# Zero rows of the latent heads' rope queries: eight ScalarE writes become eight GpSimd subtractions

## The chip, the cores and the metric

The kernel runs on one core of one Trainium2 chip. The metric is the time of one execution on the device, in microseconds (us). A core has five engines that run beside each other, each working through its own list in order: TensorE (PE, with PEld for its weight loads), VectorE (DVE), ScalarE (ACT), GpSimd (POOL) and SyncE (SP), which here issues the DMA transfers. An engine that waits for another engine's result holds up everything behind it on its own list.

## The reference

The program is a trunk of two layers over 256 latent and 256 context tokens of width 2048. The first layer joins neighbourhood attention (8 heads) with multi-head latent attention (8 heads); the second is a bidirectional gated DeltaNet. Only the latent heads matter here. With `cq` and `ckv` two normed projections of rank 512, each head computes

```
q  = rmsnorm(cq) @ w_qb          # per head: 128 columns qn, 64 columns qr
kv = rmsnorm(ckv) @ w_kvb        # per head: 128 columns kn, 128 columns v
s  = (qn . kn + rope_2d(qr) . kr) * scale      # kr: one 64-column key for all heads
o  = softmax(s) @ v
```

## The kernel before

Tokens lie along the free axis (512 columns: 256 latent, 256 context), features along the 128 partitions. Every product of fp32 data is made of three fp32r products: the operands are split into a high part (a cast on ACT, line 77 for weights) and a low part (a subtraction on DVE, line 78), and `dense` (lines 90 to 92) multiplies high by high, high by low and low by high. Weights come by DMA into four `raw` buffers.

The tile framework puts the instructions of each engine in an order of its own: it simulates the program with its own costs and lets each engine take what is ready. A change of one instruction can so move others that it has nothing to do with.

The place of the change is between the last neighbourhood head and the first latent head. In the order of the code:

- `na7 = na_head(7)` computes q, k and v of the last neighbourhood head from the layer's input `hx`. Its v product is the last reader of `hx`.
- `cx = parts_tile("cx")` takes over the buffer of `hx`. Its first half `ch` holds the high and low parts of the normed `cq` and `ckv`, eight pieces of 128x512: the high parts are cast on ACT (line 468), the low parts are subtracted on DVE (line 469). Its second half `qr` holds the rope queries of the eight heads.
- `cr.release()` gives back the buffer `craw` that lines 468 and 469 read. The pool `mr2` takes its place, and with it the three `mraw` buffers into which `adaln` loads the modulation weights of the second layer (`dn_wm`), in tiles of 512 KB. So the first of these loads waits for the last subtraction of line 469. Their products are `pmod` (line 141), two rows of TensorE's list for each tile, 16 for each of the chunks 2, 3 and 8; `macc` (line 147) and `pmt` (line 150) read a finished chunk out.
- `attend(*na7)` is the attention of head 7: scores `sp` (line 365), maximum `mx`, exponential `pr` (line 392), transposes `pt` (line 398), products `po`, in two passes (`s`).
- Then comes the loop over `j` in 0 to 3, in which the change lies. Each `j` computes the rope queries of two heads with 12 products, which read the first four pieces of `ch`, writes zeros, and calls `roped`, which scales (line 449), permutes on TensorE (`pp`, line 451), combines on DVE (lines 453 to 455) and writes the rows of each head (lines 357 and 358).

Two heads share the 128 partitions of a rope query tile. The key `kr` stands in both halves. So for each head one half of the rows of `qr` has to be zero, and line 481 writes these zeros: it reads `ones`, multiplies by 0 and writes 64 partitions x 1024 columns, twice for each `j`. The first reader of these rows is `sp<-kr,cx` of the first latent head.

Of the kernel before, what the change touches and what calls it, by code (L numbers as in the profile page):

```python
# [10 lines left out]
AF = mybir.ActivationFunctionType  # L11
ALU = mybir.AluOpType
# [6 lines left out]
T = 512  # L19
# [7 lines left out]
def trunk_kernel(ctx: ExitStack, tc: tile.TileContext, g):  # L27
    nc = tc.nc
    V, A, PE, P = nc.vector, nc.scalar, nc.tensor, nc.gpsimd
# [8 lines left out]
    def mm_tile():  # L38
        return mmp.tile([128, T], F32, name="mm", tag="mm")
# [4 lines left out]
    def cst(name, shape, src=None):  # L44
        t = const.tile(shape, F32, name=name, tag=name)
        if src is not None:
            nc.scalar.dma_start(t, src)
        return t
# [3 lines left out]
    ones = cst("ones", [128, 128])  # L52
# [32 lines left out]
    def dense(ps, w, off, kt, xh, xl, k0=0, sl=slice(0, T), first=True, last=True):  # L85
        for k in range(kt):
            c = off + k * 128
            wh, wl = w[c // 1024]
            c = slice(c % 1024, c % 1024 + 128)
            PE.matmul(ps, wh[:, c], xh[:, k0 + k, sl], start=first and k == 0, stop=False)  # L90
            PE.matmul(ps, wh[:, c], xl[:, k0 + k, sl], start=False, stop=False)  # L91
            end = PE.matmul(ps, wl[:, c], xh[:, k0 + k, sl], start=False, stop=last and k == kt - 1)  # L92
        return end.ins
# [225 lines left out]
    with tc.tile_pool(name="ab", bufs=2, reuse_waits="tile") as tp, \  # L319
# [124 lines left out]
        def roped(p, scale, parts_of):  # L444
            out = tp.tile([128, T], F32, name="rope", tag="rope", bufs=1)
            if scale == 1.0:
                A.copy(out, p)
            else:
                A.mul(out, p, scale)
            pp = ps.tile([128, S], F32, name="pp", tag="tr", bufs=TR)  # L450
            PE.matmul(pp, perm, out[:, :S], start=True, stop=True)
            t = tp.tile([128, S], F32, name="rtmp", tag="mtmp")
            V.tensor_tensor(t, pp, sinT, op=ALU.mult)
            V.tensor_tensor(out[:, :S], out[:, :S], cosT, op=ALU.mult)
            V.tensor_tensor(out[:, :S], out[:, :S], t, op=ALU.add)
            for r, hi, lo in parts_of:
                both(hi, lo, out[r])
# [5 lines left out]
        ch, qr = cx[:, 0], cx[:, 1]  # L463
        for i, gain in enumerate((q_gain, kv_gain)):
            for k in range(4):
                j = 4 * i + k
# [7 lines left out]
        rows = slice(0, 64), slice(64, 128)  # L474
        attend(*na7)
        w = load_split(g["ab_wqr"])
        for j in range(4):
            p = mm_tile()
            dense(p, w, j * 512, 4, ch, ch[:, 8:])
            for e in range(2):  # L480
                A.activation(qr[rows[1 - e], 4 * j + 2 * e:4 * j + 2 * e + 2],
                             ones[rows[1 - e], 0:1].unsqueeze(2).broadcast_to([64, 2, T]), AF.Copy, scale=0.0)
            roped(p, MLA_SCALE, [(rows[e], *[qr[rows[e], 4 * j + 2 * e + i] for i in range(2)]) for e in range(2)])
        for h in range(8):
            w = load_split(g["ab_wb"][h], 1536)
# [154 lines left out]
    with tc.tile_pool(name="dn", bufs=2, reuse_waits="tile") as tp, \  # L640
# [579 lines left out]
        for st in range(-2, 64 + LAG):  # L1220
            i, n = st // 4, st % 4
            j, m = (st - LAG) // 4, (st - LAG) % 4
# [196 lines left out]
def _program(arrays):  # L1419
    import concourse.bacc as _bacc  # L1420
    import concourse.tile as _tile

    nc = _bacc.Bacc("TRN2", target_bir_lowering=False, num_devices=1)
    g = {n: nc.dram_tensor(n, a.shape, F32, kind="ExternalInput").ap() for n, a in arrays.items()}
    g["out"] = nc.dram_tensor("out", (128, KT, S), F32, kind="ExternalOutput").ap()
    with _tile.TileContext(nc, schedule_with_timeline_sim=True) as tc:
        trunk_kernel(tc, g)
    return nc
# [11 lines left out]
```

## Time and profile before

| | us |
|---|---|
| median of 3 runs | 2490.44 (2487.42 to 2492.72) |
| the profiled execution | 2493.04 |
| its span on the core | 2491.2 |
| busy: PE / DVE / ACT / POOL | 2428.2 / 1762.8 / 1105.6 / 161.1 |

The profile is one execution. Its time is 1.8 us more than its span, and 2.6 us above the median of the runs. Times in the rows are counted from the start of the span. Busy times of PE overlap at their ends, since matmuls are pipelined.

### The profile page before, as it was taken

How to read it: one execution, taken by the hardware profiler on the slowest of the kernel's cores; microseconds unless marked ns; L12 is line 12 of the kernel's file. 1: busy time of each engine (PE TensorE's matmuls, PEld its weight loads, DVE VectorE, ACT ScalarE, POOL GpSimd, SP SyncE). 2: the span in 40 equal slices, each digit the busy share in tenths (PEclk: the TensorE clock that was granted, in tenths of full speed). 3: DMA queues.
4: the chain of work that ended last, by engine and by line, in shares of the span. 5: the costliest groups of instructions: out<-in, count | busy, mean ns of one | idle time of the engine just before them, and what ended most of it. 6: DMA issues, size and time to landing. Idle time of an engine off the chain costs nothing.

```text
span 2491.2 us, 42483 instructions
## 1 busy us (share of the span) xinstructions
PE 2428.2 (97%) x16110; PEld 1963.1 (79%) x16110; DVE 1762.8 (71%) x3538; ACT 1105.6 (44%) x2446; POOL 161.1 (6%) x165
## 2 busy tenths in 40 slices
PE   6999999999989999999999999999999999999998
PEld 4557888888858878858998989987777777777787
DVE  4654678883356687856998988885777777777765
ACT  4223332333254432257565655634444544445453
POOL 0000000000000000020011101000000000012000
PEclk9999999999999999999999999999999999999999
DMA  8872645542253366664665666774343333336454
GB/s 252 282 277 87 200 154 172 169 157 84 88 187 110 102 198 204 226 210 136 195 173 158 179 178 180 204 201 108 87 116 103 115 112 98 106 100 184 148 193 141
DMA packets 254940, 397.24 MB, mean 159 GB/s; under 512 B 122257, under 2 KB 163857, under 8 KB 254609
## 3 DMA queue, kind: packets, MB, share of 16 engines
q1 hardware_dynamic: 253584, 393.00, 52.0%
q8 instruction: 127, 2.08, 0.3%
q10 hardware_dynamic: 1152, 1.54, 0.2%
q14 instruction: 77, 0.62, 0.1%
HBM read 356.94 MB, written 35.39 MB: 157 GB/s over the span
## 4 chain that ended last, share of the span: by engine, by line
PE 88%; issue 5%; DMA 3%; DVE 2%; ACT 1%; SPq 0%; POOL 0%; DVEq 0%; POOLq 0%; ACTq 0%
PE mm L90 21%; PE mm L91 20%; PE mm L92 20%; PE pks L1033 3%; PE pmod L141 3%; PE ptr L1045 2%; PE sp L365 2%; PE mm L105 2%; PE po L365 1%; DMA mraw<-dn_wm 1%; PE ptr L1078 1%; PE psu L1064 1%; PE pks L1064 1%; PE pt L398 1%; PE mm L107 1%
## 5 line engine op out<-in xcount | busy, mean ns | idle before, releaser
L90 PE MATMUL mm<-hx,whi 128*128 128x512 f32 (+1 forms) x2304 | 843.7, 366 | 2.3 <-ACT t L664 2.2
L91 PE MATMUL mm<-hx,whi 128*128 128x512 f32 (+1 forms) x2304 | 820.6, 356 | 2.5 <-issue 2.5
L92 PE MATMUL mm<-hx,wlo 128*128 128x512 f32 (+1 forms) x2304 | 819.4, 356 | 0.6 <-DVE wlo L78 0.6
L77 ACT CAST whi<-raw 128x1024 fp32r<-128x1024 f32 (+2 forms) x346 | 338.6, 980 | 701.4 <-PE mm L91 502.3
L78 DVE TENSOR_TENSOR wlo<-raw,whi 128x1024 fp32r<-128x1024 f32 (+2 forms) x346 | 394.3, 1142 | 204.3 <-ACT whi L77 198.2
L90 PEld LDWEIGHTS mm<-hx,whi 128*128 128x128 f32 x2304 | 438.8, 190 | 106.3 <-issue 27.0
L92 PEld LDWEIGHTS mm<-hx,wlo 128*128 128x128 f32 x2304 | 438.6, 190 | 65.1 <-issue 4.2
L91 PEld LDWEIGHTS mm<-hx,whi 128*128 128x128 f32 x2304 | 438.8, 190 | 61.4 <-issue 9.2
L177 DVE SCALAR_TENSOR_TENSOR lacc<-mraw,cond,lacc 128x512 f32<-128x512 f32 x300 | 208.6, 746 | 0.7 <-DMA mraw<-dn_wm 0.7
L585 DVE SCALAR_TENSOR_TENSOR acc<-cin,taps,acc 128x508 f32<-128x508 f32 (+3 forms) x256 | 187.2, 731 | 20.3 <-ACT acc L576 17.2
L105 PE MATMUL mm<-hx,whi 128*128 128x512 f32 x480 | 173.1, 404 | 0.1
L1055 DVE SCALAR_TENSOR_TENSOR vl<-ptr,egm,vh 128x128 fp32r<-128x128 f32 x224 | 64.7, 346 | 95.1 <-ACT rf L1052 37.9
L107 PE MATMUL mm<-hx,wlo 128*128 128x256 f32 x457 | 128.4, 281 | 1.3 <-DVE wlo L1139 1.2
L141 PE MATMUL pmod<-mraw,cond 128*32 128x512 f32 (+2 forms) x640 | 98.4, 508 | 28.1 <-DMA mraw<-ab_wm 18.8
L1139 DVE TENSOR_TENSOR wlo<-raw,whi 128x1024 fp32r<-128x1024 f32 x84 | 102.5, 1221 | 13.5 <-ACT whi L1131 13.4
L105 PEld LDWEIGHTS mm<-hx,whi 128*128 128x128 f32 x480 | 88.9, 188 | 24.5 <-issue 5.0
L816 DVE SCALAR_TENSOR_TENSOR outer<-L,bv,X 128x31 f32<-128x31 f32 (+15 forms) x248 | 99.4, 401 | 6.4 <-POOL X L811 0.5
L90 PE MATMUL mm<-gx,whi 128*128 128x512 f32 x256 | 100.3, 394 | 3.4 <-DVE x1B L515 2.4
L599 ACT ACTIVATE ac<-acc 128x128 f32<-128x128 f32 x160 | 37.4, 300 | 144.2 <-DVE acc L585 144.1
L91 PE MATMUL mm<-gx,whi 128*128 128x512 f32 x256 | 100.4, 392 | 0.5 <-DVE gx L503 0.5
L92 PE MATMUL mm<-gx,wlo 128*128 128x512 f32 x256 | 99.8, 391 | 0.0
L1049 ACT ACTIVATE vh<-ptr,egm 128x128 fp32r<-128x128 f32 x224 | 71.3, 374 | 57.1 <-PE ptr L1045 55.2
(301 smaller groups left out, 3648.5 us busy)
## 6 DMA issues: line engine op xcount, KB each, us to landing
raw<-dn_w SPq DMA_DIRECT2D x194, 512.0 KB
mraw<-dn_wm SPq DMA_DIRECT2D x96, 512.0 KB
mraw<-ab_wm SPq DMA_DIRECT2D x88, 512.0 KB
raw<-ab_w SPq DMA_DIRECT2D x66, 512.0 KB
raw<-dn_wo SPq DMA_DIRECT2D x64, 512.0 KB
raw<-ab_wo SPq DMA_DIRECT2D x32, 512.0 KB
raw<-ab_w SPq DMA_DIRECT2D x32, 256.0 KB
spt<-sp SPq DMA_DIRECT2D x64, 128.0 KB
```

The source lines that it names most:

```text
L77: A.copy(hi[:, :m], raw[:, :m])
L78: V.tensor_tensor(lo[:, :m], raw[:, :m], hi[:, :m].bitcast(F32), op=ALU.subtract)
L90: PE.matmul(ps, wh[:, c], xh[:, k0 + k, sl], start=first and k == 0, stop=False)
L91: PE.matmul(ps, wh[:, c], xl[:, k0 + k, sl], start=False, stop=False)
L92: end = PE.matmul(ps, wl[:, c], xh[:, k0 + k, sl], start=False, stop=last and k == kt - 1)
L105: PE.matmul(p2, wh[:, c], x[:, :, k0 + k], start=start, stop=stop)
L107: PE.matmul(p2[:, 0], wl[:, c], x[:, 0, k0 + k], start=False, stop=False)
L141: PE.matmul(pmod[32 * q:32 * q + 32, :m], cond[:, 4 * kg + q, :], raw[c // 1024][:, half + c % 1024:half + c % 1024 + m], start=kg == 0, s ...
L177: V.scalar_tensor_tensor(acc[:, s], raw[:, q], cond[:, k, s:s + 1], acc[:, s], op0=ALU.mult, op1=ALU.add)
L585: V.scalar_tensor_tensor(o3[:, :, i0:i1], p3[:, :, i0 + d:i1 + d], taps[:, ch, t:t + 1], o3[:, :, i0:i1], op0=ALU.mult, op1=ALU.add)
L816: V.scalar_tensor_tensor(o, L[:, rows, k:k + 1].broadcast_to([128, n, m]), bv[:, k:k + 1], X[:, k:k + 1, cols].broadcast_to([128, n, m]), ...
L1139: V.tensor_tensor(w, raws[j], h.bitcast(F32), op=ALU.subtract)
```

## The change

The zeros are written by GpSimd: `ones - ones`, with the same rows and the same shape of 64x1024 (its line number is 482 in the changed kernel), instead of ACT's copy with scale 0.

```diff
             for e in range(2):
-                A.activation(qr[rows[1 - e], 4 * j + 2 * e:4 * j + 2 * e + 2],
-                             ones[rows[1 - e], 0:1].unsqueeze(2).broadcast_to([64, 2, T]), AF.Copy, scale=0.0)
+                one = ones[rows[1 - e], 0:1].unsqueeze(2).broadcast_to([64, 2, T])
+                P.tensor_tensor(qr[rows[1 - e], 4 * j + 2 * e:4 * j + 2 * e + 2], one, one, op=ALU.subtract)
```

On ACT's list, between the casts of `cx` and the scaling of the first rope query (`rope<-mm`), the rows read, with - for before and + for now:

```order
 L468 CAST cx<-craw 128x512 x8
-L481 ACTIVATE cx<-ones 64x1024 x6
 L357 CAST vt<-pv 128x512
-L481 ACTIVATE cx<-ones 64x1024
-L392 ACTIVATE pr,sm<-sp,mx 128x512
-L481 ACTIVATE cx<-ones 64x1024
-L392 ACTIVATE pr,sm<-sp,mx 128x512
+L392 ACTIVATE pr,sm<-sp,mx 128x512 x2
 L449 ACTIVATE rope<-mm 128x512
```

The eight zero writes are gone from between the casts and the two exponentials of head 7.

On GpSimd's list, between the modulation of the first layer and that of the second (`hx<-mh,hx`; `rs` belongs to a norm):

```order
 L208 TENSOR_TENSOR rs<-ms,half 128x4
 L243 TENSOR_TENSOR hx<-mh,hx 128x512 x11
-L208 TENSOR_TENSOR rs<-ms,half 128x4 x3
+L208 TENSOR_TENSOR rs<-ms,half 128x4 x2
+L482 TENSOR_TENSOR cx<-ones 64x1024 x8
+L208 TENSOR_TENSOR rs<-ms,half 128x4
 L243 TENSOR_TENSOR hx<-mh,hx 128x512 x11
```

The eight writes stand there in one piece; only the first has a wait, for TensorE.

On TensorE's list, what follows the products of `j` = 0 and 1 was before:

```order
L141 MATMUL pmod<-mraw,cond 32x512 x4
L365 MATMUL sp<-kT,qT 128x256 x3
L398 MATMUL pt<-ident,pr 128x128 x4
L141 MATMUL pmod<-mraw,cond 32x512 x2
L365 MATMUL sp<-kT,qT 128x256 x3
```

Now the second pass's scores and the twelve products of `j` = 2 stand there, and behind these:

```order
L398 MATMUL pt<-ident,pr 128x128 x8
L141 MATMUL pmod<-mraw,cond 32x512 x4
L365 MATMUL po<-PT,vt 128x256
L141 MATMUL pmod<-mraw,cond 32x512 x2
L398 MATMUL pt<-ident,pr 128x128 x2
L365 MATMUL po<-PT,vt 128x256 x11
```

So the first modulation products moved behind the scores, the products of `j` = 2 and eight transposes. Before the second `pp` (the permutation of `j` = 1) TensorE had ten tiles of `pmod` and now has eight; up to the first scores of the first latent head it had 16 and now has 15. DVE's list is unchanged from the splits of the weights through the eight subtractions of line 469. Farther on the lists differ again in small pieces, mostly at the start of the second layer, where ACT's list now holds two more loads of function tables.

## Rows read from the trace of the kernel before

**Rows 1.** The page, part 1: busy time, share of the span, instructions.

```profile
PE 2428.2 (97%) x16110; PEld 1963.1 (79%) x16110; DVE 1762.8 (71%) x3538; ACT 1105.6 (44%) x2446; POOL 161.1 (6%) x165
```

**Rows 2.** Busy time by stretch; last three columns: granted clock, DMA share, GB/s.

```profile
690.00:700.00 10.00, 5.74 (x24) 4.05 (x23) 6.41 (x12) 9.92 (x14) 0.00 (x0) 1.00 0.36 118
700.00:710.00 10.00, 9.40 (x36) 4.43 (x36) 4.28 (x11) 5.67 (x12) 0.00 (x0) 0.83 0.76 265
710.00:720.00 10.00, 9.42 (x51) 4.49 (x50) 4.27 (x11) 1.70 (x5) 0.00 (x0) 1.00 0.53 166
720.00:730.00 10.00, 8.10 (x38) 3.67 (x38) 5.63 (x11) 4.61 (x7) 0.00 (x0) 1.00 0.70 226
...
1140.00:1150.00 10.00, 8.67 (x90) 7.84 (x89) 6.30 (x10) 8.03 (x21) 2.63 (x4) 1.00 0.54 165
```

**Rows 3.** Instructions in order of time: start us, us, engine, what.

```profile
687.40 0.39 PE L92 MATMUL mm<-hx,wlo 128*128 128x512 f32 x1
...
688.85 1.22 DVE L78 TENSOR_TENSOR wlo<-raw,whi 128x1024 fp32r<-128x1024 f32 x1
...
690.91 1.88 DVE L469 TENSOR_TENSOR cx<-craw,cx 128x512 fp32r<-128x512 f32 x3
...
693.32 3.09 DVE L469 TENSOR_TENSOR cx<-craw,cx 128x512 fp32r<-128x512 f32 x5
693.32 6.39 ACT L481 ACTIVATE cx<-ones 64x1024 fp32r<-64x1024 f32 x6
...
696.56 0.39 PE L92 MATMUL mm<-cx,wlo 128*128 128x512 f32 x1
...
700.60 3.12 PE L141 MATMUL pmod<-mraw,cond 128*32 128x512 f32 x8 [3.65 <-DMA mraw<-dn_wm]
...
701.28 0.69 ACT L392 ACTIVATE pr<-sp,mx 128x512 f32<-128x512 f32 x1
...
723.84 0.70 PE L451 MATMUL pp<-rope,ropet 128*128 128x256 f32 x2
```

**Rows 4.** The chain that ended last: start us, us, what.

```profile
696.48 3.98 DMA mraw<-dn_wm
...
717.65 1.01 PE pmod L141 x4
...
737.62 0.23 PE mm L91
...
741.80 2.97 PE sp L365 x12
```

**Rows 5.** GpSimd's groups by shape: busy us, mean ns, idle before.

```profile
L820 POOL TENSOR_TENSOR X<-X,bv 128x1024 f32<-128x1024 f32 x7 | 14.4, 2051 | 95.2 <-DVE X L818 95.2
...
L1185 POOL TENSOR_TENSOR hx<-re,hx 128x1024 fp32r<-128x1024 f32 x4 | 9.7, 2414 | 10.3 <-ACT hx L1184 10.3
...
L810 POOL MEMSET X<- 128x1024 f32 x8 | 7.7, 960 | 67.7 <-DVE bv L809 36.7 <-DMA sums<-gts 31.0
```

**Rows 6.** In order of time: GpSimd and DVE at three places.

```profile
1092.99 1.31 POOL L243 TENSOR_TENSOR hx<-mh,hx 128x512 fp32r<-128x512 f32 x1 [0.41 <-ACT mh L241]
1093.30 0.48 DVE L235 SCALAR_TENSOR_TENSOR mh<-x1B,Am,rb 128x256 f32<-128x256 f32 x1
...
1356.15 1.92 POOL L820 TENSOR_TENSOR X<-X,bv 128x1024 f32<-128x1024 f32 x1 [20.24 <-DVE X L818]
1357.13 2.01 DVE L78 TENSOR_TENSOR wlo<-raw,whi 128x1024 fp32r<-128x1024 f32 x1 [1.06 <-ACT whi L77]
...
2238.41 2.37 POOL L1185 TENSOR_TENSOR hx<-re,hx 128x1024 fp32r<-128x1024 f32 x1 [6.74 <-ACT hx L1184]
2239.80 1.54 DVE L585 SCALAR_TENSOR_TENSOR acc<-cin,taps,acc 128x508 f32<-128x508 f32 x1
2239.80 4.33 DVE L585 SCALAR_TENSOR_TENSOR acc<-cin,taps,acc 128x508 f32<-128x508 f32 x2
2240.74 2.83 POOL L1185 TENSOR_TENSOR hx<-gin,hx 128x1024 fp32r<-128x1024 f32 x1
```

**Rows 7.** In order of time, ACT at the start of the second layer.

```profile
1129.65 1.28 ACT L596 ACT_TABLE_LOAD   x1 [2.49 <-DVE acc L585]
```

## The prediction

> **What bounds the kernel now.** I read the page's part 1 first: TensorE is busy for 97% of the span [rows 1], so a time is lost or won where TensorE waits. Next the busy time by stretch around the change. Between 690 and 730 us PE is busy for 5.74, 9.40, 9.42 and 8.10 of each 10 us [rows 2], so 7.3 us stand idle; that is all that the change could win here. The instructions in order of time tell why: PE ends the products of `j` = 0 and 1 at 696.95, and its next row is `pmod`, which waits 3.65 us for its weights, until 700.60 [rows 3]. In the chain that ended last this is 3.98 us of transfer from its issue at 696.48 [rows 4]. The issue comes 0.07 us after the last of the eight subtractions of line 469 has ended (693.32 + 3.09 = 696.41) [rows 3], as the buffers demand. In the same time ACT is full (9.92 of 10 us [rows 2]): six zero writes take 6.39 us [rows 3], 1.06 us each, 8.5 us for eight, and the exponentials of head 7 start only at 701.28 behind them. So two things meet at 700: a transfer released by DVE, and ACT's zero writes. The first ends last for `pmod`.
>
> **The change part by part.** *Removed:* 8.5 us of ACT. The exponentials can start when the casts of `cx` are over, some 7 us earlier. Alone this would let PE pass over the 3.65 us, since the scores, twelve products and eight transposes now stand in front of `pmod`.
>
> *Added:* eight GpSimd operations in one piece, free to start when the last product of `hx` has ended, 687.40 + 0.39 = 687.8 [rows 3]. Nothing needs their result before the first latent head, 741.80 [rows 4]. Their own duration is so hidden. What is not hidden is what they do to DVE. The trace of before shows three pairs [rows 6]. At 1356.15 GpSimd starts a product; DVE's split of line 78, which takes 1.22 us elsewhere [rows 3], starts at 1357.13 and takes 2.01: it ends 1.07 us after GpSimd's end at 1358.07. At 2239.80 a DVE operation of 508 columns starts within one GpSimd operation and takes 1.54 us, ending at 2241.34, 0.56 after GpSimd's 2240.78; the GpSimd operation behind it takes 2.83 instead of 2.37; the next DVE operation ends at 2244.13, 0.56 after that one's end at 2243.57. At 1093.30 a DVE operation that reads one operand from PSUM (`rb`) takes its usual 0.48 inside a GpSimd operation. I read from this that a DVE operation with two inputs in SBUF and a GpSimd operation with two inputs exclude each other, whole operation by whole operation, and take turns.
>
> The Trainium skill (GPSIMD Engine Reference, 8. Key points) says that GpSimd shares its SBUF interfaces with VectorE, with contention for DVE instructions that have two SBUF inputs; it gives no price. The rows go further than the rule: the DVE operation is not slowed but held to the end. If the two merely shared the cycles, nine DVE operations would last twice as long at most, some 6 us more instead of the 11.4 below, and the sum would be about 0.
>
> Line 78 and all eight of line 469 (`craw` and `cx`) have two SBUF inputs, and they are DVE's next nine of this kind after 687.8. So they alternate with the eight zero writes:
>
> - A zero write's duration isn't in the trace. Bounds are 0.96 us (a MEMSET of 1024 columns, no input) and 2.41 (a subtraction of 1024 dense columns to fp32r) [rows 5]. I take 1.92, the undisturbed `X<-X,bv` [rows 6], the only row with a repeated operand. One that had to let DVE go first runs 0.14 less behind it (2.23 of 2.37 [rows 6]): 1.78.
> - First zero write 687.8 to 689.7; line 78 ends 1.07 later, 690.8, not at 690.07. Then seven turns of 1.78 + 0.56 = 2.34 us: the fourth subtraction ends at 700.2, the seventh at 707.2, the eighth, alone again, 0.62 later (3.09 / 5 [rows 3]) at 707.8. Before it was 696.41. The added wait is 11.4 us.
> - Behind these on DVE stand the split of `vt`, the reciprocals and scalings of head 7's probabilities, on which PE's transposes wait. I put these at some 2 us, so the transposes are done about 711.
> - PE needs the fourth subtraction for `j` = 0 and 1, so it drags until 700.2 and has 15 products of 0.23 [rows 4] left, then scores and twelve more products: about 707.5, then the wait for the transposes.
> - The first weights are issued at 707.9 and, with the 4.1 us of before (696.48 to 700.60), arrive at 712.0. Now the transfer is late again, 11.4 us later than before, although PE reaches it later in its list.
> - Chunk 2 has eight tiles. Three buffers keep the queue filled, and at the 265 GB/s of the stretch at 700 [rows 2] a tile of 524288 bytes takes 1.98 us: 712.0 + 7 x 1.98 + 1.0 for the last product (a tile takes 1.0 [rows 4]) = 726.9.
> - From the second `pp` (723.84 [rows 3]) to the first latent scores (741.80 [rows 4]) before took 18.0 us with six tiles of `pmod`. Now the same products stand there with seven tiles, 19.0: the scores start at 745.9. That is 4.1 later, and one tile (15 instead of 16) is still to be done: 1.0. Sum: **5.1 us slower**.
>
> From 730 on PE has no idle time to take this back until the next stage, whose buffers are released by the heads' last products, so I carry it to the end. The granted clock in 700 to 710 is 0.83 [rows 2], behind PE's 3.65 us of idling: part of that stretch ran at 1.2 instead of 2.4 GHz. The changed kernel idles longer; since it waits for transfers then, I add nothing, and 2 us to the upper end.
>
> Profiled time 2493.0 + 5.1 = 2498.1. The profile stands 2.6 above the median of the runs; a run is so predicted at 2490.4 + 5.1 = 2495.5 us.
>
> Each 0.1 us of a zero write counts eight times: at 0.96 the sum is 5.1 - 7.7 = -2.6, at 2.41 it is 5.1 + 3.9 = 9.0. The skill's page on GpSimd (3.1 Elementwise) measures 4497 ns for two inputs of 2048 columns; half of it, an estimate of 2.25 us, would make the sum 7.7. The trace's dense 2.41 agrees with that, its row with a repeated operand does not.
>
> *Moved, later:* at the start of the second layer ACT has two more table loads of 1.28 us [rows 7], while PE's order puts more products ahead of a transfer for which it idled (8.67 of 10 us busy [rows 2]). I take 0, with bounds of -1.3 (that idle time gone) and +2.6 (both loads in PE's way).
>
> **Rivals.**
> 1. *The two engines don't hold each other* for these writes, which touch only 64 partitions and read one element over and over. Then DVE ends at 696.4 as before, the weights are there at 700.6, and PE comes to them after 0.9 + 2.8 + 0.9 us of scores, products and transposes (the first and last are estimates from the same kinds of products) at 701.5 instead of 712.0: 5.1 - 10.5 = -5.4, 2485.0 us. It stays under the 7.3 us of idle time. For it: no row has such operands. Against: every pair of two-input operations that overlaps in this trace shows the hold.
> 2. *Shorter zero writes:* with both operands repeated a write takes about 1.4 us (as much below 1.92 as that is below 2.41). The sum is 5.1 - 4.2 = +0.9, 2491.3 us, no difference. The same end comes about if the engines share the cycles instead of taking turns (6 us of delay: 5.1 - 5.4 = -0.3). For it: a repeated operand goes with a shorter time in the rows [rows 5]. Against: only one line says so, and the three pairs show turns [rows 6].
> 3. *Dense price:* 2.25 to 2.41 us each, with DVE's later work and the low clock on top: +8 to +11, about 2499.5. For it: the same operation and the same output type as line 1185.
>
> **How the numbers follow.** A measurement of this kernel can tell about 0.2%, 5.0 us, from no change. The forecast (1.7 to 2.1 us each, sums from +3 to +7) has 0.40, a little over half of it beyond 5.0. Rival 3 has 0.27, rival 2 has 0.21, rival 1 has 0.12. Slower: 0.23 + 0.27 + a rest of rival 2 with the loads of tables 0.02 = 0.52. Same: 0.17 + 0.18 = 0.35. Faster: 0.12 and a little of rival 2 = 0.13. The range for eight in ten runs from 2487.5 (rival 2 with the later gain, and part of rival 1) to 2501.5 (the dense price with the low clock); the forecast's own is 2493.5 to 2497.5.
>
> **What would show it.** In the changed profile GpSimd should show eight operations of 64x1024 from 687.8 on, one ending every 2.3 us, the last near 705.4; line 469 should show operations of about 2.3 us instead of 0.68; the first `mraw` issue should stand near 708 and the first `pmod` near 712; ACT's exponentials of head 7 near 694 and 699; the first latent scores near 746. If line 469 keeps 0.68 us, rival 1 holds and PE idles under 3 us between 690 and 730. If all this is seen but the end isn't later, a stage behind 880 has absorbed it and my carrying it to the end is wrong.

## The result, and the profile after

The changed kernel takes 2497.12 us (median of 14 runs, 2488.93 to 2500.97), the kernel before 2492.18 (14 runs, 2487.42 to 2494.88). The medians lie 4.9 us apart. The ratio of the times is 1.0023, with a 95% interval from 1.0014 to 1.0032: 5.7 us slower. Timed again later beside a control it was 1.0014 (1.0000 to 1.0027), 3.5 us. So the change costs some 3 to 6 us.

The profiled execution of after is the fastest of its 14 (2488.93 us, span 2487.2), and ends 4 us before the profiled one of before. The two ends can't be compared therefore; stretches can, as below. At 687 us its times stand 0.4 us earlier than those of before.

Part 1 of the page of after answers to [rows 1]:

```profile
PE 2423.6 (97%) x16110; PEld 1959.2 (79%) x16110; DVE 1772.2 (71%) x3538; ACT 1099.8 (44%) x2440; POOL 177.4 (7%) x173
```

Busy time by stretch (us, PE, PEld, DVE, ACT, POOL, then granted clock, DMA share, GB/s), as in [rows 2]:

```profile
690.00:700.00 10.00, 6.27 (x20) 4.46 (x20) 10.00 (x9) 4.83 (x11) 9.70 (x5) 0.83 0.15 52
700.00:710.00 10.00, 5.70 (x30) 4.37 (x29) 9.98 (x12) 1.70 (x4) 5.91 (x3) 0.97 0.15 36
710.00:720.00 10.00, 8.34 (x28) 3.46 (x28) 2.14 (x6) 1.40 (x5) 0.00 (x0) 0.52 0.86 287
720.00:730.00 10.00, 8.58 (x40) 3.35 (x39) 5.58 (x13) 2.48 (x5) 0.00 (x0) 1.00 0.57 184
```

PE stands idle for 11.1 of these 40 us, not 7.3. ACT is no longer full, DVE now is; and the DMA queues, which moved 265 GB/s in the stretch at 700, move 36 until 710. In the order of time, beside [rows 3] (start us, us, engine, what):

```profile
687.54 18.52 POOL L482 TENSOR_TENSOR cx<-ones 64x1024 fp32r<-64x1024 f32 x8 [37.57 <-PE mm L92]
688.45 2.06 DVE L78 TENSOR_TENSOR wlo<-raw,whi 128x1024 fp32r<-128x1024 f32 x1
691.37 6.04 DVE L469 TENSOR_TENSOR cx<-craw,cx 128x512 fp32r<-128x512 f32 x3
697.93 9.28 DVE L469 TENSOR_TENSOR cx<-craw,cx 128x512 fp32r<-128x512 f32 x5
707.28 1.28 SPq L136 DMA_DIRECT2D mraw<-dn_wm  x3
708.71 1.42 PE L398 MATMUL pt<-ident,pr 128*128 128x128 f32 x8 [4.30 <-DVE pr L395]
711.18 3.24 PE L141 MATMUL pmod<-mraw,cond 128*32 128x512 f32 x8 [1.05 <-DMA mraw<-dn_wm]
728.29 0.70 PE L451 MATMUL pp<-rope,ropet 128*128 128x256 f32 x2
748.17 1.21 PE L365 MATMUL sp<-kT,qT 128*128 128x512 f32 x4
```

Eight GpSimd writes in 18.52 us are 2.31 each. The same eight subtractions of line 469 that took 5.0 us in [rows 3] now take 15.3, and end at 697.93 + 9.28 = 707.21. The issue of the first `mraw` follows 0.07 us later, as before. The chain that ended last (start us, us, what) is to be read beside [rows 4]:

```profile
688.45 2.06 DVE wlo L78
690.51 0.60 DVE mx L389
691.45 5.96 DVE cx L469 x3
698.01 9.21 DVE cx L469 x5
708.14 7.37 DMA mraw<-dn_wm
```

In [rows 4] the transfer, the first of the weights, begins at 696.48; now the chain has the third of them, and all three are issued behind 15 us of line 469.

One turn of the two engines, taken from the same stretch:

```profile
692.33 2.23 POOL L482 TENSOR_TENSOR cx<-ones 64x1024 fp32r<-64x1024 f32 x1
692.73 2.38 DVE L469 TENSOR_TENSOR cx<-craw,cx 128x512 fp32r<-128x512 f32 x1
694.64 2.22 POOL L482 TENSOR_TENSOR cx<-ones 64x1024 fp32r<-64x1024 f32 x1
695.03 2.38 DVE L469 TENSOR_TENSOR cx<-craw,cx 128x512 fp32r<-128x512 f32 x1
```

GpSimd ends at 694.56; DVE, started at 692.73, ends at 695.11, 0.55 later. GpSimd's next, started at 694.64, ends at 696.86, 1.75 behind DVE's end. Each runs only when the other is through, as in the pairs of [rows 6].

### The profile page after: what moved, and what is told of

Read it like the earlier page. It is cut to its first block, busy times and chain, and to the rows that moved or that the text cites. A ratio compares the mean times of both kernels' runs of the same rounds, so it can differ in the third digit from the quotient of the medians.

```text
span 2487.2 us, 42484 instructions
## 1 busy us (share of the span) xinstructions
PE 2423.6 (97%) x16110; PEld 1959.2 (79%) x16110; DVE 1772.2 (71%) x3538; ACT 1099.8 (44%) x2440; POOL 177.4 (7%) x173
## 4 chain that ended last, share of the span: by engine, by line
PE 87%; issue 5%; DVE 3%; DMA 3%; ACT 1%; SPq 0%; POOL 0%; DVEq 0%; POOLq 0%; ACTq 0%
PE mm L90 21%; PE mm L91 20%; PE mm L92 20%; PE pks L1033 3%; PE pmod L141 3%; PE ptr L1045 2%; PE sp L365 2%; PE mm L105 2%; PE po L365 1%; PE ptr L1078 1%; DMA mraw<-dn_wm 1%; PE psu L1064 1%; PE pks L1064 1%; PE mm L107 1%; PE pt L398 1%
## 5 line engine op out<-in xcount | busy, mean ns | idle before, releaser
L585 DVE SCALAR_TENSOR_TENSOR acc<-cin,taps,acc 128x508 f32<-128x508 f32 (+3 forms) x256 | 186.7, 730 | 19.9 <-ACT acc L576 17.0
```

Of the source, the lines that this page charges most:

```text
L585: V.scalar_tensor_tensor(o3[:, :, i0:i1], p3[:, :, i0 + d:i1 + d], taps[:, ch, t:t + 1], o3[:, :, i0:i1], op0=ALU.mult, op1=ALU.add)
```

## The experiments

The theory: a GpSimd operation with two inputs and a DVE operation with two inputs in SBUF hold each other, and this makes line 469, and by it the first weights, late. The main rival: the new order of the lists costs the time. Four kernels have the changed kernel's order on every engine and differ only in what GpSimd does at this place, so the order is ruled in or out by them; a fifth (the one cut in quarters) keeps the order too, with more GpSimd operations. For all kernels, counted from the start of DVE's first `sp<-sp,bias` of the stretch (688.51 in the profile of before, 688.11 in that of after), in us:

| kernel | line 469 ends | first `pmod` | first latent scores | ratio (95%) |
|---|---|---|---|---|
| before (two profiles) | 7.9, 7.9 | 12.1, 12.1 | 53.2, 54.9 | 1 |
| same lists as before (two) | 7.9, 7.9 | 11.9, 12.0 | 57.6, 53.6 | 1.0011 (1.0000 to 1.0023); 0.9995 (0.9986 to 1.0005) |
| after (three profiles) | 19.1, 19.1, 19.1 | 23.1, 23.1, 23.1 | 60.1, 58.8, 58.2 | 1.0023; 1.0014 |
| four writes early, four late | 12.9 | 17.9 | 54.3 | 1.0013 (0.9997 to 1.0029) |
| quarters | 11.0 | 15.0 | 49.7 | 0.9985 (0.9974 to 0.9996) |
| one input | 10.0 | 15.1 | 49.3 | 0.9991 (0.9980 to 1.0002) |
| memset | 7.9 | 12.7 | 48.7 | 0.9981 (0.9968 to 0.9993) |
| all eight late | 7.9 | 13.0 | 47.7 | 0.9987 (0.9976 to 0.9998) |
| ACT, behind each `j` | 7.9 | 12.7 | 50.0 | 0.9969 (0.9956 to 0.9982) |
| before plus GpSimd writes | 7.9 | 11.9 | 55.0 | 1.0000 (0.9988 to 1.0012) |

**All eight late.**

```diff
-                one = ones[rows[1 - e], 0:1].unsqueeze(2).broadcast_to([64, 2, T])
+                one = ch[rows[1 - e], 15, 0:1].bitcast(F32).unsqueeze(2).broadcast_to([64, 2, T])
```

> All eight GpSimd subtractions stay, but their operands are one element of the last low part that line 469 writes, so they cannot start before line 469 is through; the order of every engine's list is that of the changed kernel. Exclusion of the two engines (my theory): line 469 takes 0.6 to 0.7 us an operation again and ends near 696, the first mraw issue stands near 696 and the first latent scores near 738 to 741, 8 to 10 us before those of the changed kernel; the writes now meet fewer two-input operations of DVE (line 455, one split), which may cost 1 us. Time 7 to 9 us under the changed kernel, ratio to before 0.997 to 0.999. Rival, the new order of the lists costs the time: ratio 1.002 as the changed kernel, whatever line 469 does. Rival, the writes themselves end too late for someone: they end 9 us later than in the changed kernel, so the ratio is 1.003 or more.

With the same lists and the same eight writes, started after line 469, the scores come 10.4 to 12.3 us before those of the changed kernel, more than I expected, and the ratio falls by 0.0036 (9 us; 0.0027 against the second timing). The rival of the order falls. Groups of this kernel's stretch (what, count, busy us, mean ns):

```profile
L482 POOL TENSOR_TENSOR cx<-cx 64x1024 fp32r<-64x1024 f32 x8 | 15.7, 1956 | 46.7 <-PE mm L92 46.2
L469 DVE TENSOR_TENSOR cx<-craw,cx 128x512 fp32r<-128x512 f32 x8 | 5.0, 686 | 0.0
L395 DVE TENSOR_SCALAR pr<-pr,rc 128x512 f32<-128x512 f32 x2 | 3.1, 1603 | 0.0
L78 DVE TENSOR_TENSOR wlo<-raw,whi 128x512 fp32r<-128x512 f32 x1 | 2.0, 2042 | 0.0
L358 DVE TENSOR_TENSOR PT<-pt,PT 128x512 fp32r<-128x512 f32 x2 | 1.4, 678 | 0.0
```

In the kernel before, lines 395 and 78 read in the order of time (start us, us, engine, what):

```profile
702.29 0.49 DVE L395 TENSOR_SCALAR pr<-pr,rc 128x512 f32<-128x512 f32 x1
705.63 0.68 DVE L78 TENSOR_TENSOR wlo<-raw,whi 128x512 fp32r<-128x512 f32 x1
```

The writes now hold line 78 (2.04 instead of 0.68) and also line 395, which reads one tile in SBUF, scaled by one number a row (1.60 instead of 0.49). Line 358, with one operand in PSUM, keeps its 0.68.

**Four early, four late.**

```diff
+                one = (ones if j < 2 else ch[:, 15].bitcast(F32))[rows[1 - e], 0:1] ...
```

> The first four GpSimd subtractions are free to start early as in the changed kernel, the last four wait for the last of line 469; order of the lists as in the changed kernel. Exclusion in turns: four turns of 2.3 us and then DVE alone, so that line 469 ends near 702.5 (between 696 and 707) and the first latent scores near 743; time about half way between the kernel before and the changed one, ratio 1.000 (0.9985 to 1.001). Rival, the new order: 1.002. Rival, GpSimd as a whole slows DVE by shared cycles, without turns: line 469 slower by a constant share in the overlap and not in steps of a whole GpSimd operation.

Line 469 shows the step, three held operations and then five alone:

```profile
691.31 6.04 DVE L469 TENSOR_TENSOR cx<-craw,cx 128x512 fp32r<-128x512 f32 x3
697.88 3.08 DVE L469 TENSOR_TENSOR cx<-craw,cx 128x512 fp32r<-128x512 f32 x5
```

It ends at 700.96 (12.9 in the table; I expected 702.5, with four turns on line 469; one of the four fell on line 78, in 2.06 us). The scores lie between all early and all late. The ratio, 1.0013, is higher than I expected, and its interval tells it from neither the kernel before nor the changed one.

**One input.**

```diff
-                P.tensor_tensor(..., one, one, op=ALU.subtract)
+                P.tensor_scalar(..., one, 0.0, None, op0=ALU.mult)
```

> The eight GpSimd writes multiply the one element by a constant 0 (one SBUF input instead of two), at the same place and in the same order of the lists. If only GpSimd operations with two SBUF inputs hold DVE: line 469 keeps 0.6 to 0.7 us, ends near 696, ratio to before 0.997 to 0.999. If any GpSimd operation that reads SBUF holds it: turns as in the changed kernel, about 1.8 + 0.6 us each or shorter if one input makes the write shorter (1.0 to 1.9 us); line 469 ends near 702 to 707, ratio 1.000 to 1.0025.

Neither of the two cases as I put them. The writes are longer (2.77 us), and yet line 469 ends only 2.1 us late. One pair:

```profile
694.35 2.77 POOL L482 TENSOR_SCALAR cx<-ones 64x1024 fp32r<-64x1024 f32 x1
694.81 1.12 DVE L469 TENSOR_TENSOR cx<-craw,cx 128x512 fp32r<-128x512 f32 x1
```

DVE ends at 695.93, in the middle of GpSimd's operation and 1.58 us behind its start. Alone it needs 0.68; if it ran undisturbed once it was let go, it got going at 695.25, 0.9 us behind GpSimd's start. Two more rows bear this out: line 78, which comes 0.89 us behind the write that starts at 688.65, keeps its usual 1.22, and line 469 beside the write that starts at 691.50 also ends 1.58 us behind that start:

```profile
689.54 1.22 DVE L78 TENSOR_TENSOR wlo<-raw,whi 128x1024 fp32r<-128x1024 f32 x1
691.62 1.46 DVE L469 TENSOR_TENSOR cx<-craw,cx 128x512 fp32r<-128x512 f32 x1
```

So this operation holds DVE for its first third only.

**Memset.**

```diff
+                P.memset(qr[rows[1 - e], 4 * j + 2 * e:4 * j + 2 * e + 2].bitcast(F32), 0.0)
```

> The eight GpSimd writes are memsets of 0 without any input, at the same place and in the same order of the lists. My theory (two inputs on both engines): no hold, line 469 ends near 696, writes of 0.5 to 1.0 us each, ratio to before 0.997 to 0.999. If any GpSimd operation that uses SBUF holds DVE: turns of 0.5 to 1.0 + 0.6 us, line 469 ends near 700, ratio 0.999 to 1.001. Rival, the new order of the lists: 1.002.

```profile
L482 POOL MEMSET cx<- 64x1024 f32 x8 | 7.6, 948 | 37.9 <-PE mm L92 37.6
L469 DVE TENSOR_TENSOR cx<-craw,cx 128x512 fp32r<-128x512 f32 x8 | 5.0, 686 | 0.0
```

The memsets stand in the midst of line 469, which doesn't see them. As expected, and the kernel is faster than before: 0.9981.

The Trainium skill (SBUF — State Buffer, "SBUF: two separate sides") says that DVE and GpSimd share a port pair by an exclusive lock which the one that starts first keeps "for the whole instruction", and that it concerns DVE operations in a 2-port mode, or with two SBUF inputs against a GpSimd operation that reads SBUF. The memset, which reads nothing, agrees with it (line 469 keeps 686 ns); the held line 395 (1603 ns) does if it runs in a 2-port mode, which no row says; the one-input write, which lets DVE go after some 0.9 of 2.77 us, doesn't.

**Quarters.**

```diff
+                for q in range(4): P.tensor_tensor(...[:, q // 2:q // 2 + 1, q % 2 * 256:q % 2 * 256 + 256], ...)
```

> Each of the eight GpSimd subtractions is cut into four of 64x256, 32 in all, from the same point; the order of every list is that of the changed kernel. Turns by whole operations (my theory): each of DVE's nine two-input operations waits for one short write only, a turn of about 0.5 + 0.6 = 1.1 us instead of 2.3, so that line 469 ends near 700.5 (between 699 and 702), 6 to 7 us before the changed kernel, though GpSimd is busy for as long or longer; first latent scores 741 to 743; ratio to before 0.998 to 1.000. Rival, GpSimd's total time counts (shared cycles, or DVE pushed back by the bytes that GpSimd moves): line 469 ends near 707 again, ratio 1.002.

```profile
L482 POOL TENSOR_TENSOR cx<-ones 64x256 fp32r<-64x256 f32 x32 | 23.6, 766 | 38.1 <-PE mm L92 37.6
L469 DVE TENSOR_TENSOR cx<-craw,cx 128x512 fp32r<-128x512 f32 x8 | 7.9, 1048 | 0.0
```

GpSimd is busy for longer than in the changed kernel (23.6 against 18.0 us), and DVE's operations take 1.05 us instead of 1.97. What DVE pays is the length of one GpSimd operation, not their sum: shared cycles are out. With the start of each profile taken off, line 469 ended 8.1 us before the changed kernel's, where I expected 6 to 7.

**ACT, one write ahead of each latent head.**

```diff
+            A.activation(qr[rows[1 - h % 2], 2 * h:2 * h + 2], ones[rows[1 - h % 2], 0:1] ..., AF.Copy, scale=0.0)
             attend(*o, 8 + h, None, ...)
```

> No GpSimd writes: ACT writes the zeros as in the kernel before, but one 64x1024 write ahead of each latent head's attention instead of eight ahead of head 7's exponentials. TensorE's list around the first modulation products stands as in the kernel before (products of the modulation ahead of the scores). If ACT's eight writes in one piece were the cost in the kernel before: exponentials of head 7 start near 693 and 698 instead of 701, and the first latent scores come 2 to 5 us earlier than before, ratio 0.998 to 0.999. Rival, the order of TensorE's list is what decides, and with the old one it waits 3.65 us for the first weights as before: less than 1 us won, ratio 0.9995 to 1.0005.

The edit moved nothing: every engine's list is in the same order as in the kernel before, with six of the writes in one piece again.

```profile
694.93 6.39 ACT L489 ACTIVATE cx<-ones 64x1024 fp32r<-64x1024 f32 x6
702.89 0.69 ACT L392 ACTIVATE pr<-sp,mx 128x512 f32<-128x512 f32 x1
```

So it says nothing about where ACT's writes should stand, and the gain from freeing ACT isn't separated here from the gain of the new order; it serves as a control. Its 1.0011 gives the scatter of a ratio, and its scores at 57.6 show how far one execution can differ in this stretch. So I timed control and change together:

> The kernel whose ACT writes were moved in the code to the latent heads, but which has every engine's list in the same order as the kernel before: a control. If 1.0011 was scatter, the ratio now is between 0.9990 and 1.0010; if something of this kernel that the lists do not show costs time, 1.001 again.

> The changed kernel once more, timed beside a control. My theory: 1.002 again (1.001 to 1.003), first latent scores 58.5 to 60.5 us after DVE's first line 387 of the stretch, line 469 ending 19.1 after it. Rival, its loss was the scatter between executions and chips: ratio within 0.0010 of the control's.

Control 0.9995 (0.9986 to 1.0005), change 1.0014 (1.0000 to 1.0027): 0.0019 or 4.7 us apart, almost twice what the rival allows; the two intervals overlap a little. The scores came at 58.2, just short of the range. With the kernels above, which take the loss away by the hold alone, the loss is the change's; its size is known to about 2 us.

**The two kernels once more.**

> The kernel before once more, for a second profile of it: which of the differences behind the place of the change (3.0 us of waiting for weights at 904, the low clock near 1075, the stall near 1311, the low clock near 1645) belong to the kernel and which to one execution. If they belong to the kernel, each stands at the same place again within 0.5 us; if they are chance, the offsets against the first profile differ by 2 to 5 us behind 1075. Up to 745 no difference over 0.5 us.

> The changed kernel once more, for a second profile of it. My theory: the first latent scores 6 to 7 us later than before again, line 469 ending near 707 again; behind 1075 the offsets against the kernel before vary by some us from one execution to the next. If the early end of the first profile of the changed kernel (4.6 us before that of the kernel before) belonged to the kernel, this one would end there again.

Around the change the second profile of after repeats the first (line 469 at 19.1); its scores come 3.9 us later than those of before again, less than the 6 to 7 expected. The scores of before again come 1.7 us later than those of the first profile, where I expected no difference over 0.5 up to there. Behind 1075 chance rules, and the second profile of after doesn't repeat the early end: its span is 3.2 us longer than the first's. Where the first profile of before lost most, its row of the busy times by stretch is:

```profile
1310.00:1320.00 10.00, 7.66 (x72) 6.02 (x59) 6.00 (x13) 1.16 (x2) 1.04 (x2) 0.66 0.51 149
```

The same stretch in the second profile of before:

```profile
1310.00:1320.00 10.00, 10.00 (x67) 9.11 (x66) 9.62 (x22) 6.40 (x9) 1.04 (x2) 1.00 0.51 138
```

PE's idling and the lower clock at 1310 belong to one execution. There the profile of after gains 4.8 us on the first of before, and 2.6 more near 1650; at 1000 it had still been 5.5 us behind, with the start taken off.

**GpSimd writes added to the kernel before.**

```diff
                 A.activation(qr[...], ..., AF.Copy, scale=0.0)
+                P.tensor_tensor(qr[...], one, one, op=ALU.subtract)
```

> The kernel before, whose ACT zero writes all stay, and behind each a GpSimd subtraction that writes the same zeros once more; each waits for ACT's write of the same rows, so they start near 694.4, when three of line 469's operations are left. The order of TensorE's, DVE's and ACT's lists up to the latent heads is that of the kernel before. My theory (the hold costs in any order): three turns of 2.3 us, line 469 ends near 701.5 instead of 696.4, the first weights come 5 us later, and the scalings of head 7's probabilities (one SBUF input) are held as well; first latent scores 5 to 8 us later than before, ratio 1.002 to 1.003. Rival, the changed kernel loses by its new order of lists: no loss here, ratio 0.9995 to 1.0005.

A miss. GpSimd's first write came in the midst of line 469 and had to wait for all that was left of it:

```profile
694.45 3.65 POOL L484 TENSOR_TENSOR cx<-ones 64x1024 fp32r<-64x1024 f32 x1 [44.14 <-ACT cx L481]
694.46 0.69 DVE L469 TENSOR_TENSOR cx<-craw,cx 128x512 fp32r<-128x512 f32 x1
695.06 0.69 DVE L469 TENSOR_TENSOR cx<-craw,cx 128x512 fp32r<-128x512 f32 x1
695.66 0.69 DVE L469 TENSOR_TENSOR cx<-craw,cx 128x512 fp32r<-128x512 f32 x1
```

3.65 is 1.90 of waiting, to DVE's end at 696.35, and 1.75, what a write that had to wait takes in the changed kernel too. Here three DVE operations went by in a row, where in the changed kernel one did; why the turns didn't set in is open. The seven later writes do hold DVE (the scalings of line 395 take 1.97 and 1.30 us), the ratio is 1.0000, and the scores come at 55.0, among those of the kernel before. Here the hold by itself costs nothing that can be measured; it did where it made line 469 late, for which the path waits.

**ACT, behind each `j`.**

```diff
             roped(p, MLA_SCALE, ...)
+            for e in range(2):
+                one = qr[rows[1 - e], 4 * j + 3 - 2 * e, 0:1].bitcast(F32).unsqueeze(2).broadcast_to([64, 2, T])
+                A.activation(qr[rows[1 - e], 4 * j + 2 * e:4 * j + 2 * e + 2], one, AF.Copy, scale=0.0)
```

> No GpSimd writes: ACT writes the zeros, but reads an element of a rope query of the same j that is written first, so that two writes stand behind each j's casts instead of eight ahead of head 7's exponentials. My theory: line 469 ends near 696, head 7's exponentials come near 693 and 698, TensorE's list is that of the changed kernel at this place, and ACT has room later (2 to 5 of each 10 us busy): first latent scores 3 to 6 us earlier than before, ratio 0.998 to 0.999, as with the memsets. Rival, ACT's 8.5 us cost wherever they stand: ratio 1.000.

```profile
693.48 0.69 ACT L392 ACTIVATE pr<-sp,mx 128x512 f32<-128x512 f32 x1
711.39 2.13 ACT L483 ACTIVATE cx<-cx 64x1024 fp32r<-64x1024 f32 x2 [0.77 <-DVE cx L358]
721.06 2.13 ACT L483 ACTIVATE cx<-cx 64x1024 fp32r<-64x1024 f32 x2
727.96 2.13 ACT L483 ACTIVATE cx<-cx 64x1024 fp32r<-64x1024 f32 x2
738.73 2.23 ACT L483 ACTIVATE cx<-cx 64x1024 fp32r<-64x1024 f32 x2
```

The same ACT work, two writes behind the casts of each `j`, is the fastest of all at 0.9969; its interval overlaps that of the memsets. TensorE's order is that of the changed kernel up to the first `pmt`, and differs in small pieces behind it. At the scores 4.8 us are won, as expected; the ratio says 7 to 8, and where the rest comes from no run shows. Both versions beat both kernels.

## Why the prediction was right

The forecast was 5.1 us slower; measured were 5.7 and, again, 3.5. The mechanism is the forecast one: turns of the two engines make line 469 late, and line 469 the first weights. That the sum came so close is in part luck: errors in it cancel, as the second and the third point show.

- *The hold* is as the steps had it. A free write took 1.89 us (I took 1.92), a turn 2.3 (2.34). Line 78 ended at 690.51 (690.8), line 469 at 707.21 (707.8), the first issue stood at 707.28 (707.9), the first `pmod` at 711.18 (712.0); take 0.4 off mine for the earlier start, and all lie within 0.4 us. The rule that I read from the pairs was too narrow, though: line 395, with one input, is held too, and a GpSimd write with one input holds DVE for some 0.9 us. For these eight writes and nine operations it made no difference.
- *The sum at the scores.* The two kernels with line 469 unheld and the changed order have their scores at 48.2 on the mean, the four profiles with the lists of before at 54.8: -6.6, where rival 1's price at the scores was 4.1 - 10.5 = -6.4. The changed kernel's three stand at 59.0, 10.8 behind the unheld; I had 10.5. So the change is +4.2, where I had +4.1. But the forecast scores, 57.4 on this scale, came 0.8 to 2.7 us later, and those of before, of which I had only an early profile (53.2), lie 1.6 later on the mean too. The two errors cancel.
- *Mis-sized: the wait and the clock.* I had the 10.5 us as PE's waiting, and added nothing to the sum for the clock, and 2 us to the upper end, on the ground that PE waits for transfers then. The stretch from DVE's first `sp<-sp,bias` to the scores shows how it is made up, in the changed kernel and in the one with all writes late (us, PE, PEld, DVE, ACT, POOL, then granted clock, DMA share, GB/s):

```profile
688.11:748.17 60.06, 47.63 (x200) 26.47 (x198) 40.78 (x59) 21.39 (x42) 17.42 (x8) 0.89 0.48 158
689.03:736.75 47.72, 41.84 (x200) 24.40 (x198) 37.05 (x59) 21.30 (x42) 15.65 (x8) 1.00 0.61 199
```

PE idles for 12.4 us against 5.9, and for the same products in the same order it is busy for 47.6 against 41.8, at a granted clock of 0.89 against 1.00. Over all profiles of these kernels (12.4 against 6.0 of idling, 46.6 against 42.2 of work) 6.4 us of the 10.8 are waiting, where I had 10.5, and 4.4 are longer work, for which I had nothing. That the lower clock makes the work longer is read from these rows; no run isolates it. The unheld kernels idle for 5.8 and 6.1 us between 690 and 730, where rival 1 had PE idle under 3.

- *The end of chunk 2* shows the same. I put it at 726.9; it ended at 727.30 + 1.05 = 728.35. The stretch at 710 ran at a granted clock of 0.52, nearly all of it at 1.2 GHz, after PE had idled for 8 of the 20 us before. The third tile took 1.92 us there, where a tile takes 1.05 at the full clock:

```profile
715.55 1.92 PE L141 MATMUL pmod<-mraw,cond 128*32 128x512 f32 x4 [0.62 <-DMA mraw<-dn_wm]
```

Its buffer was free, and the sixth load issued, at 717.51; in the second profile of after, whose stretch at 710 stood at 0.82, at 715.34. So a slow PE also frees buffers late. From the second `pp` to the scores it took 19.9 us in the first profile, where I had 19.0.

- *The tile still to do* showed itself: between 800 and 820 all three profiles of after fall back by 1.1 to 1.2 us more against the first of before. I had 1.0.
- *Carried to the end:* at 1000 the three profiles of after stand 5.5, 5.8 and 3.6 us behind the first of before, with the start taken off, and four with the lists of before at 0, 1.0, 2.2 and -2.3; on the mean the change is 4.7 us behind. So it is carried through the first layer. Behind this no single profile can show it; the medians do.
- *The second layer's new order*, taken at 0, can't be told from chance: its two further table loads [rows 7] are there, and their price is below the scatter of some 2 us.

Rival 1 falls with the turns; rival 2's short write and rival 3's dense price fall with the 1.89, and rival 2's shared cycles with the quarters. For a write without input rival 1 would have been right: the memsets hold nothing.

## What to carry to other kernels

Work given to GpSimd is hidden only if DVE isn't held by it: look at which DVE operations stand beside it, and whether a DMA or PE waits for one of them. Here a memset or a later start by a data dependency took the hold off line 469, and shorter operations made it shorter; leaving the work on its engine and moving it behind what the path needs did as well. Time that TensorE loses to a late transfer may cost more than the wait, if the clock granted behind it is lower: here 4.4 us beside 6.4. And a difference of 0.2% isn't to be read from the ends of two profiles.

## What was not expected of the hardware

- A DVE operation with a single SBUF input (line 395, 0.49 us) was held like one with two: 1.10 to 2.11 us in the kernel with all writes late.
- The one-input GpSimd write (2.77 us) was longer than the two-input one (1.89) and held DVE for some 0.9 us only.
- A GpSimd write that came upon a run of DVE operations waited 1.90 us for the rest of one and three more; in the changed kernel the two took turns.
